# Down projection: 16 of its 22 k tiles as 7 of 8 block products, with the intermediate sums added to x1 by DMA

## The chip, the cores and the metric

One core of a Trainium2 chip runs the kernel. The metric is the device time of one execution in microseconds. Before the change it is 732.96 us, the median of 3 runs (732.8 to 734.33).

## The reference

One encoder layer over 512 positions of width 1024, all in float32. Only its last part matters here:

```python
h2 = rmsnorm(x, g_ffn)
x  = x + (silu(h2 @ w_gate) * (h2 @ w_up)) @ w_down      # w_down: 2816 x 1024
y  = rmsnorm(x, g_final)
```

Ahead of it stand an input projection, differential attention, retention in two directions, two gates and an output projection that gives the residual stream x1. The down projection is `act @ w_down`, with act of 512 x 2816: 22 k tiles of 128 along the contraction.

## The kernel before

**Split operands.** Every float32 operand of a matmul is split into a high part h (a cast to float32r, on ScalarE) and a low part l (source minus h, on VectorE). A product then takes three matmuls (h x h, h x l, l x h), all into one PSUM bank; `mm3` issues them. A weight unit is 128 x 1024: it is loaded into a buffer w_r (9 of them), cast to w_h and subtracted to w_l (4 pairs of buffers). `conv_gen` does that up to three units ahead of the matmul that uses them.

**Feed-forward groups.** `strassen` computes gate and up products of 2 x 2 blocks with seven block products in place of eight, in the order 1, 7, 6, 4, 5, 2, 3. Each product adds onto one of three pairs of banks, Y, Z and X; the intermediate values that later combinations need are copied out of PSUM by ScalarE (`snap_gen`), and the next product onto the same bank waits for that copy. The weight side of a product is a block (a, c, d) or a sum of blocks. Of the sums, t + x and s + v are formed in the buffer by an accumulating DMA issued on GpSimd's queue (POOL), t + a and t + c by a VectorE addition. Groups 0 to 4 have two units per product, group 5 is half as wide and has one. A full product is 24 matmuls of 512 columns.

**Down projection before.** For each of the 22 k tiles, one activation tile (act, 128 x 512, split into act_h and act_l by `actsplit_gen`) and one weight unit are multiplied into eight banks pd, four row tiles by two column halves: 24 matmuls per k tile. The last four k tiles run bank by bank, so that each bank ends early enough for its end work: `x2_gen` adds the bank to x1t on VectorE, then squares and gains, `final_gen` normalizes and stores.

**The order of the work** on every engine is fixed when the program is written: the class `Streams` keeps a clock for each engine with a cost for each kind of instruction, and steps the generator whose next instruction could start first; ties go to the lower rank. Each engine then runs its own queue in that order and waits on semaphores. So an instruction that is put into a queue stands in front of all that follows, whether or not it is urgent.

**Names.** fY, fZ and fX are the banks of a feed-forward group; fa4_0 to fa4_3 its four activation tiles for group 4, which `actT_gen` transposes into banks aT on the matmul engine; fg, snap_z and snap_v are values in between. S1 to S7 are the split parts that stand in for the activation side of a product. Line 90 (91 after) issues matmuls, 120 (121) casts and copies, 125 (126) VectorE additions and subtractions, 131 (132) operations with three operands, 168 (169) accumulating DMAs.

Of the kernel before, what the change touches and what calls it, by code (L numbers as in the profile page):

```python
# [36 lines left out]
class Streams:  # L37
# [184 lines left out]

@with_exitstack
def block_kernel(ctx: ExitStack, tc: tile.TileContext, xT, w_st, w_v, w_g, w_up, w_o, w_f, w_fl,
                 w_d, gc, gf, vec, cosT, sinT, posd, negd, y):

# [60 lines left out]
    for g in range(GROUPS):  # L287
        for p in PRODUCTS:
            units += [(g, p, u) for u in range(n_units(g))]
    units += [w_d[k] for k in range(FT)]  # L290
    raw, conv = {}, {}
    used = [0]
    AHEAD = 3

    def blk(g, b, u):
        return w_fl[b] if g == GROUPS - 1 else w_g[int(g[1]), b, u] if isinstance(g, str) else w_f[g, b, u]

    WARM = 9

# [552 lines left out]

    def x1t_gen():

        yield lambda: len(x1s) == KT and ("S", 0) in done
# [55 lines left out]
    def actT_gen(g, w):  # L911
        yield lambda: all((g, i) in AT for i in range(NT))
        for j in range(w // P):
            ps = yield from psum("o", f"aT{g}_{j}")
            yield from E.transposes([(ps[:, i * P:(i + 1) * P], AT[g, i][:, j * P:(j + 1) * P]) for i in range(NT)], ident)
            t = slot(f"act{g}_{j}")
            yield from E.copy(t, ps)
            E.release("o", ps)
            act32[4 * g + j] = t

    act32, usedk = {}, [0]

    def actsplit_gen():
        for k in range(FT):
            yield lambda: k in act32 and "ffn" in done and k <= usedk[0] + AHEAD
            acts[k] = yield from split(act32[k], f"act{k}")


    banks = ("w", "w", "w", "mm", "mm", "mm", "o", "o")
    gfs = []  # L930

    def gf_gen():
# [7 lines left out]
    def x2_gen(i, hf, ps, ss):  # L940

        t, u = x1t[i, hf], slot(f"u{i}{hf}")
        n = 2 if hf and i == NT - 1 else 1
        w = T // n
        for c in range(n):
            cs = slice(c * w, (c + 1) * w)
            yield from E.tt(t[:, cs], ps[:, cs], t[:, cs], ALU.add)
            if c == n - 1:
                E.release(banks[2 * i + hf], ps)
# [60 lines left out]
            for i in range(2):  # L1010
                E.spawn(v_evac_gen(pss[i], name, 2 * g + i), 15)

    def strassen(g, S, evac):

        nu = n_units(g)
        w = T * nu // 2
        per = 2 if nu == 2 else 4
        bank = {}
        for p in PRODUCTS:
            key = {"6": "n", "5": "v2", "3": "v4", "4": "z"}.get(p)  # L1020
            c = {"1": "Y", "6": "Y", "5": "Y", "3": "Y", "7": "Z", "4": "Z", "2": "X"}[p]
            first = p in "172"
            us = []
            for t in range(2):
                tag = {"Y": "mm", "Z": ("mm", "w")[t], "X": "w"}[c]
                if first:
                    bank[c, t] = (yield from psum(tag, f"f{c}{g}_{t}"))[:, :w]
                if key:
                    yield have((g, key, t))
                ps = bank[c, t]  # L1030
                for i in range(4):
                    if len(us) == i // per:
                        us.append((yield from take()))
                    uh, ul = us[i // per]
                    cs = slice((i % per) * w, (i % per + 1) * w)
                    yield lambda: (p, i) in S
                    sh, sl = S[p, i]
                    ts_ = slice(t * P, (t + 1) * P)
                    yield from E.mm3(ps, sh[:, ts_], sl[:, ts_], uh[:, cs], ul[:, cs], first and i == 0, i == 3, not first)
                    if t == 1 and i % per == per - 1:  # L1040
                        drop(us[i // per])
                if p in "1765":
                    E.spawn(snap_gen((g, {"1": "n", "7": "z", "6": "v2", "5": "v4"}[p], t), ps, w), 20)
                evac(p, t, ps, tag, w)
            if p == "7":
                done.add(("S", g))

    def main_gen():
        ps0 = []
# [101 lines left out]
        pd = {}  # L1151
        wt = {}

        def down(i, hf, k, last):
            b = 2 * i + hf
            if b not in pd:
                pd[b] = yield from psum(banks[b], f"pd{b}")
# [5 lines left out]
            yield from E.mm3(pd[b], ah[:, ts_], al[:, ts_], wt[k][0][:, cs], wt[k][1][:, cs], k == 0, last)  # L1163

        FIRST = 2
        for part in range(2):
            for k in range(FIRST):
                for i in range(2 * part, 2 * part + 2):
                    for hf in range(2):
                        yield from down(i, hf, k, False)  # L1170
                if part:
                    drop(wt.pop(k))
                    usedk[0] += 1
        for k in range(FIRST, FT - TAIL):
            for i in range(NT):
                for hf in range(2):
                    yield from down(i, hf, k, False)
            drop(wt.pop(k))
            usedk[0] += 1
        for i in range(NT):  # L1180
            ss = small([P, 3 if i == NT - 1 else 2], f"ss3_{i}")
            for hf in range(2):
                for k in range(FT - TAIL, FT):
                    yield from down(i, hf, k, k == FT - 1)
                E.spawn(x2_gen(i, hf, pd[2 * i + hf], ss), 10)
            E.spawn(final_gen(i, ss), 10)

    E.spawn(warm_gen(), 0)
# [82 lines left out]
```

## Time and profile before

| | |
|---|---|
| median of 3 runs | 732.96 us (732.8 to 734.33) |
| the profiled execution | 733.82 us, span 732.0 us |
| matmul engine (PE) | busy 715.3 us, 98% of the span, 3332 matmuls |
| VectorE (DVE) | 499.7 us, 68% |
| ScalarE (ACT) | 461.3 us, 63% |
| GpSimd (POOL) | 90.6 us, 12% |
| DMA | 98.65 MB, mean 135 GB/s |
| down projection | from 602.63 us to the last matmul, which starts at 724.26 |

A time line names engine, line, operation and tiles; a bracket at the end of a row gives how long the engine was idle before it and which engine ended that wait. The bar of a matmul is modelled and overlaps the next one, so the distance from start to start tells what it takes. On VectorE and ScalarE too, a row may begin a little before the bar of the last one ends.

### The profile page before, as it was taken

Reading aid. Unit: us, or ns where it says so; the run is one execution under the profiler, and the core shown is the slowest. Engines: PE = TensorE matmul, PEld = TensorE weight load, DVE = VectorE, ACT = ScalarE, POOL = GpSimd, SP = SyncE. Lnnn points to the kernel's source line nnn. Section 1 sums busy time; section 2 is a strip of 40 time slices with the busy share of each in tenths; the row PEclk is TensorE's granted clock in tenths of the full one; section 3 lists DMA queues with packets and bytes.
Section 4 is the critical chain, followed back from the end, with each engine's and each line's share of the span. In section 5 each row is a group of like instructions: output and inputs, shape, how many; then the busy total and the mean of one; then the engine's idle time right before and its main releaser. Section 6 shows DMA issues by size and latency. Waiting matters only on the chain.

```text
span 732.0 us, 9022 instructions
## 1 busy us (share of the span) xinstructions
PE 715.3 (98%) x3332; PEld 577.9 (79%) x3332; DVE 499.7 (68%) x704; ACT 461.3 (63%) x738; POOL 90.6 (12%) x109
## 2 busy tenths in 40 slices
PE   9989999999989999999999999999999999999995
PEld 7867677777768878887888888888888898888884
DVE  6678787779867478887577677676676864323345
ACT  7679897597696667666468866565656564223233
POOL 4261321011024002100000101000000000000000
PEclk9999999999999999999999999999999999999998
DMA  9801110311236438767604939586675563230002
GB/s 319 322 24 56 59 57 30 116 51 64 88 115 188 129 115 239 250 203 187 156 17 130 233 110 258 116 227 177 172 201 167 178 201 116 87 115 0 1 7 109
DMA packets 29052, 98.65 MB, mean 135 GB/s; under 512 B 3504, under 2 KB 3504, under 8 KB 29008
## 3 DMA queue, kind: packets, MB, share of 16 engines
q1 hardware_dynamic: 22752, 76.04, 30.3%
q0 software_dynamic: 5968, 21.50, 14.2%
q8 instruction: 26, 0.43, 0.2%
q10 hardware_dynamic: 288, 0.52, 0.2%
q14 instruction: 18, 0.15, 0.1%
HBM read 95.96 MB, written 2.10 MB: 134 GB/s over the span
## 4 chain that ended last, share of the span: by engine, by line
PE 87%; ACT 7%; DVE 4%; issue 1%; DMA 0%; SPq 0%; ACTq 0%; DVEq 0%
PE pd L90 16%; PE fY L90 15%; PE fZ L90 8%; PE wo L90 6%; PE up L90 6%; PE fYg L90 5%; PE fX L90 4%; PE pfirst L90 3%; PE rg L90 3%; PE rv L90 3%; PE fZg L90 3%; PE dv L90 2%; PE fXg L90 1%; PE s L99 1%; PE ao L90 1%; PE aT L108 1%
## 5 line engine op out<-in xcount | busy, mean ns | idle before, releaser
L125 DVE TENSOR_TENSOR w_l<-w_r,w_h 128x1024 fp32r<-128x1024 f32 (+1 forms) x66 | 76.1, 1157 | 84.3 <-ACT w_h L120 84.2
L120 ACT CAST w_h<-w_r 128x1024 fp32r<-128x1024 f32 (+1 forms) x66 | 65.6, 996 | 90.0 <-PE pd L90 61.8
L90 PE MATMUL fY<-w_h,S 128*128 128x512 f32 (+1 forms) x384 | 117.4, 376 | 0.0
L90 PEld LDWEIGHTS fY<-w_h,S 128*128 128x128 f32 x384 | 70.4, 188 | 12.1
L90 PE MATMUL fY<-w_l,S 128*128 128x512 f32 (+1 forms) x192 | 71.4, 372 | 0.0
L90 PE MATMUL pd<-w_h,act_l 128*128 128x512 f32 x176 | 68.6, 390 | 0.5 <-DVE act_l L125 0.5
L90 PE MATMUL pd<-w_l,act_h 128*128 128x512 f32 x176 | 68.6, 390 | 0.1
L90 PE MATMUL pd<-w_h,act_h 128*128 128x512 f32 x176 | 68.7, 390 | 0.0
L90 PE MATMUL fZ<-w_h,S 128*128 128x512 f32 (+1 forms) x192 | 58.9, 377 | 0.0
L90 PEld LDWEIGHTS fY<-w_l,S 128*128 128x128 f32 x192 | 36.2, 189 | 5.7
L90 PEld LDWEIGHTS fZ<-w_h,S 128*128 128x128 f32 x192 | 35.4, 188 | 6.1
L90 PEld LDWEIGHTS pd<-w_h,act_l 128*128 128x128 f32 x176 | 33.0, 188 | 7.7 <-DVE act_l L125 0.9
L90 PEld LDWEIGHTS pd<-w_l,act_h 128*128 128x128 f32 x176 | 33.0, 188 | 7.2 <-DVE w_l L125 0.6
L90 PEld LDWEIGHTS pd<-w_h,act_h 128*128 128x128 f32 x176 | 33.0, 188 | 6.8
L90 PE MATMUL fZ<-w_l,S 128*128 128x512 f32 (+1 forms) x96 | 35.6, 371 | 0.0
L90 PE MATMUL fYg<-w_h,S 128*128 128x512 f32 x96 | 31.0, 391 | 0.0
L90 PE MATMUL fX<-w_h,S 128*128 128x512 f32 (+1 forms) x96 | 28.5, 371 | 0.0
L115 ACT ACTIVATE fg<-fg,r 128x512 f32<-128x512 f32 (+1 forms) x24 | 16.2, 684 | 18.4 <-DVE fg L125 18.4
L90 PE MATMUL wo<-m_h,w_h 128*128 128x512 f32 x64 | 25.4, 397 | 0.0
L90 PE MATMUL wo<-m_l,w_h 128*128 128x512 f32 x64 | 25.1, 392 | 0.3 <-DVE m_l L125 0.2
L90 PE MATMUL wo<-m_h,w_l 128*128 128x512 f32 x64 | 24.9, 389 | 0.0
L149 DVE TENSOR_REDUCE mx<-s 128x1 f32<-128x512 f32 x32 | 21.2, 681 | 4.6 <-PE s L99 4.4
(498 smaller groups left out, 1833.5 us busy)
## 6 DMA issues: line engine op xcount, KB each, us to landing
w_r<-w_d SPq DMA_DIRECT2D x22, 512.0 KB, 3.4
w_r<-w_st SPq DMA_DIRECT2D x12, 512.0 KB, 4.5
w_r<-w_v SPq DMA_DIRECT2D x8, 512.0 KB, 5.9
w_r<-w_up SPq DMA_DIRECT2D x8, 512.0 KB, 3.3
w_r<-w_o SPq DMA_DIRECT2D x8, 512.0 KB, 4.3
x<-xT SPq DMA_DIRECT2D x8, 256.0 KB, 5.4
w(g_a)_r<-w_g SPq DMA_DIRECT2D x4, 512.0 KB, 3.7
w(g_t)_r<-w_g SPq DMA_DIRECT2D x4, 512.0 KB, 3.8
```

The source lines that it names most:

```text
L90: self.nc.tensor.matmul(out, lhsT=lhsT, rhs=rhs, start=start, stop=stop, skip_group_check=more)
L99: self.nc.tensor.matmul(outs[i % 2], lhsT=lhsT, rhs=rhs, start=i < 2, stop=i >= len(ops) - 2)
L108: self.nc.tensor.transpose(out=out, in_=in_, identity=identity)
L115: self.nc.scalar.activation(out, in_, func, **kw)
L120: self.nc.scalar.copy(out=out, in_=in_)
L125: (self.nc.vector if eng == "dve" else self.nc.gpsimd).tensor_tensor(out=out, in0=a, in1=b, op=op)
L149: self.nc.vector.tensor_reduce(out=out, in_=a, axis=AX.X, op=op, **kw)
```

## The change

The first 16 k tiles become two groups, d0 and d1, of eight k tiles each. Each is a 2 x 2 block product done with `strassen`: the four row tiles and the eight k tiles are halved, and the weight blocks lie in a new array w_db, prepared ahead of the launch. `dblocks_gen` makes the seven activation-side parts from eight act tiles (28 splits of 128 x 256 and 16 additions or subtractions of 128 x 256 per group): those of d0 during group 5, those of d1 during d0. `down_evac_gen` copies an intermediate bank out of PSUM into a tile cd, with its sign, and adds that tile to x1t by an accumulating DMA on POOL's queue: 12 such copies and adds in d0, 8 in d1. Bank pair X stays and takes d1's product 2 on top of d0's; d1 puts Y into the two banks of tag o. The last six k tiles (REST) run as all 22 did before, onto six banks that d1 leaves and two new ones. Since rows of the lower half are formed with their sign turned, the act tiles from 16 on have their second half negated, and `x2_gen` subtracts for row tiles 2 and 3.

```diff
+REST = 6
...
-    units += [w_d[k] for k in range(FT)]
+    units += [(g, p, u) for g in ("d0", "d1") for p in PRODUCTS for u in range(2)]
+    units += [w_d[k] for k in range(REST)]
...
-    def dma_add(self, out, in_):
-        yield "pool", [out]
+    def dma_add(self, out, in_, sbuf_in=False):
+        yield "pool", [out, in_] if sbuf_in else [out]
         self.nc.gpsimd.dma_start(out=out, in_=in_, accum_op=ALU.add)
...
+    def dblocks_gen(g):
+        k0 = 8 * int(g[1])
+        prev = "d0" if g == "d1" else GROUPS - 1
+        store = Sd[g]
+        yield lambda: all(k0 + n in act32 for n in range(8))
+        a = [act32.pop(k0 + n) for n in range(8)]
+        w, w2 = {}, {}
+        yield have(("P", prev - 1, "2") if g == "d0" else ("P", prev, "1"))
+        for i in range(4):
+            yield from part(store, "1", i, a[i][:, A])
+        for i in range(4):
+            w[i] = slot(f"dsum{g}{i}")
+            yield from E.tt(w[i][:, A], a[i][:, A], a[i][:, B], ALU.add)
+            yield from part(store, "7", i, w[i][:, A])
...
+    def down_evac_gen(g, p, t, ps, tag):
+        key, i, hf, op = {"1": ("n", t, 0, ALU.subtract), "7": ("z", 2 + t, 1, ALU.add), "6": ("v2", 2 + t, 0, ALU.add),
+                          "4": (None, 2 + t, 0, ALU.subtract), "5": ("v4", 2 + t, 1, ALU.subtract),
+                          "3": (None, t, 1, ALU.add), "2": (None, 0, 0, None)}[p]
+        if key or op and g == "d0":
+            c = slot(f"c{g}{p}{t}")
+            if op == ALU.add:
+                yield from E.copy(c, ps)
+            else:
+                yield from E.act(c, ps, AF.Copy, scale=-1.0)
+            if key:
+                done.add((g, key, t))
+            else:
+                E.release(tag, ps)
+            yield from E.dma_add(x1t[i, hf], c, sbuf_in=True)
...
+        bank = {}
+        for g in ("d0", "d1"):
+            def evac(p, t, ps, tag, w):
+                E.spawn(down_evac_gen(g, p, t, ps, tag), 9)
+            if g == "d1":
+                for c in "YZ":
+                    for t in range(2):
+                        bank.pop((c, t))
+            yield from strassen(g, Sd[g], evac, TAGS if g == "d0" else {**TAGS, "Y": ("o", "o")}, bank)
+        pd = {(t, 0): bank["X", t] for t in range(2)}
+        pd.update({(t, 1): bank["Y", t] for t in range(2)})
+        pd.update({(2 + t, 0): bank["Z", t] for t in range(2)})
+        wt, onto = {}, set(pd)
...
-        for k in range(FIRST, FT - TAIL):
+        for k in range(FT - REST, FT - TAIL):
```

In the program's order the matmul engine's queue goes from 3317 rows to 3269, VectorE's from 704 to 796. Up to the end of group 4 the queues are the same.

VectorE's queue at the end of group 4, where group 5's first units are split and combined (w139, w140, w(5_0_t)) and the last two activation tiles of group 4 are made (fa4_0, fa4_1), before:

```order
L125 TENSOR_TENSOR w139_l_5311<-w(5_0_t)_r_5139,w139_h_5310 128x1024
L125 TENSOR_TENSOR w(5_0_t)_r_5139<-w(5_0_t)_r_5139,w(5_0_a)_r_5093 128x1024
L131 SCALAR_TENSOR_TENSOR fa4_0_5321<-fY4_0_5017,r2_95,fg4_0_5278 128x512
L125 TENSOR_TENSOR w140_l_5332<-w(5_0_t)_r_5139,w140_h_5331 128x1024
L125 TENSOR_TENSOR w(5_0_t)_r_5139<-w(5_0_t)_r_5139,w(5_0_c)_r_5179 128x1024
L131 SCALAR_TENSOR_TENSOR fa4_1_5341<-fY4_1_5038,r2_95,fg4_1_5301 128x512
```

and now:

```order
L126 TENSOR_TENSOR w139_l_5314<-w(5_0_t)_r_5139,w139_h_5313 128x1024
L126 TENSOR_TENSOR w(5_0_t)_r_5139<-w(5_0_t)_r_5139,w(5_0_a)_r_5093 128x1024
L126 TENSOR_TENSOR S1_0_5299<-act0_0_4071,S1_0_5299 128x256
L126 TENSOR_TENSOR S1_1_5341<-act0_1_4085,S1_1_5341 128x256
L126 TENSOR_TENSOR S1_2_5344<-act0_2_4097,S1_2_5344 128x256
L132 SCALAR_TENSOR_TENSOR fa4_0_5325<-fY4_0_5017,r2_95,fg4_0_5277 128x512
L126 TENSOR_TENSOR w140_l_5336<-w(5_0_t)_r_5139,w140_h_5335 128x1024
L126 TENSOR_TENSOR w(5_0_t)_r_5139<-w(5_0_t)_r_5139,w(5_0_c)_r_5179 128x1024
L126 TENSOR_TENSOR S1_3_5348<-act0_3_4114,S1_3_5348 128x256
L126 TENSOR_TENSOR dsumd00_5385<-act0_0_4071 128x256
L132 SCALAR_TENSOR_TENSOR fa4_1_5352<-fY4_1_5038,r2_95,fg4_1_5300 128x512
```

Five rows of d0's parts now stand ahead of fa4_1.

VectorE's queue where the weights for product 4 of d0 are made (units w151 and w152; S2, S1 and dsum are parts of d0 and d1), after the change:

```order
L132 SCALAR_TENSOR_TENSOR w151_l_5816<-w(d0_0_t)_r_5261,w151_h_5815 128x1024
L126 TENSOR_TENSOR w(d0_1_t)_r_5302<-w(d0_1_t)_r_5302,w(d0_1_c)_r_5399 128x1024
L126 TENSOR_TENSOR S2_1_5836<-act1_1_4409,S2_1_5836 128x256
L126 TENSOR_TENSOR S2_2_5867<-act1_2_4421,S2_2_5867 128x256
L126 TENSOR_TENSOR S2_3_5870<-act1_3_4438,S2_3_5870 128x256
L126 TENSOR_TENSOR dsum2d00_5694<-act1_0_4395,dsumd00_5385 128x256
L126 TENSOR_TENSOR S1_3_5838<-act2_3_4762,S1_3_5838 128x256
L126 TENSOR_TENSOR dsumd10_5881<-act2_0_4719 128x256
L132 SCALAR_TENSOR_TENSOR w152_l_5857<-w(d0_1_t)_r_5302,w152_h_5856 128x1024
```

Between the addition into w(d0_1_t) and w152_l stand six rows of parts. VectorE's queue around the units of the same numbers before the change:

```order
L125 TENSOR_TENSOR w151_l_5769<-w151_r_5408,w151_h_5768 128x1024
L125 TENSOR_TENSOR act7_l_5805<-act1_3_4438,act7_h_5804 128x512
L125 TENSOR_TENSOR w152_l_5803<-w152_r_5465,w152_h_5802 128x1024
L125 TENSOR_TENSOR act8_l_5839<-act2_0_4719,act8_h_5838 128x512
L125 TENSOR_TENSOR w153_l_5837<-w153_r_5499,w153_h_5836 128x1024
```

There, splits of weights (w_l) and of activation tiles (act_l) alternate, without an addition.

POOL's queue in d0, after the change (cd06 and cd04 are the copies of products 6 and 4, the last digit the half; before, the queue ends with the two loads of gf):

```order
L169 DMA x1t20_3851<-cd060_5842 128x512
L169 DMA x1t30_3903<-cd061_5865 128x512
L169 DMA x1t20_3851<-cd040_5907 128x512
L169 DMA w(d1_0_t)_r_5889<-w_db 128x1024
L169 DMA w(d1_1_t)_r_5936<-w_db 128x1024
L169 DMA x1t30_3903<-cd041_5934 128x512
```

The accumulating loads of d1's weights stand behind adds into x1t; the second add into x1t20 may be issued only when the first has landed.

## Rows read from the trace of the kernel before

**Rows 1.** The page, busy us of each engine with its share of the span
```profile
PE 715.3 (98%) x3332; PEld 577.9 (79%) x3332; DVE 499.7 (68%) x704; ACT 461.3 (63%) x738; POOL 90.6 (12%) x109
```

**Rows 2.** Stretches of 40 us: a feed-forward group, the down projection; columns in its head
```profile
core 0: us, PE busy (x) PEld busy (x) DVE busy (x) ACT busy (x) POOL busy (x), PEclk, DMA share, GB/s
468.00:508.00 40.00, 40.00 (x186) 33.14 (x186) 27.87 (x30) 23.59 (x32) 3.49 (x4) 1.00 0.68 185
604.00:644.00 40.00, 40.00 (x181) 33.07 (x181) 15.06 (x19) 14.39 (x21) 0.00 (x0) 1.00 0.32 106
```

**Rows 3.** The chain of waits: start us, us, what
```profile
558.70 5.44 PE fZ L90 x24
...
585.30 0.44 PE aT L108 x4
...
588.39 2.88 PE fY L90 x24
...
605.81 96.62 PE pd L90 x426
```

**Rows 4.** Time line of PE: start us, us, what, idle before it and releaser
```profile
583.68 0.55 PE L108 MATMUL aT<-ident,fa 128*128 128x128 f32 x3 [0.24 <-DVE fa L131]
...
602.63 0.40 PE L90 MATMUL pd<-w_h,act_h 128*128 128x512 f32 x1
602.86 0.40 PE L90 MATMUL pd<-w_l,act_h 128*128 128x512 f32 x1
603.73 0.50 PE L90 MATMUL pd<-w_h,act_l 128*128 128x512 f32 x1 [0.47 <-DVE act_l L125]
```

**Rows 5.** Time line of DVE at the end of group 4
```profile
575.05 0.69 DVE L125 TENSOR_TENSOR fg<-fX,snap_n 128x512 f32<-128x512 f32 x1 [1.22 <-PE fX L90]
575.66 1.22 DVE L125 TENSOR_TENSOR w_l<-w(5_0_a)_r,w_h 128x1024 fp32r<-128x1024 f32 x1
576.79 1.22 DVE L125 TENSOR_TENSOR w_l<-w(5_0_t)_r,w_h 128x1024 fp32r<-128x1024 f32 x1
578.05 1.23 DVE L125 TENSOR_TENSOR w(5_0_t)_r<-w(5_0_t)_r,w(5_0_a)_r 128x1024 f32<-128x1024 f32 x1
579.19 0.74 DVE L131 SCALAR_TENSOR_TENSOR fa<-fY,r,fg 128x512 f32<-128x512 f32 x1
580.47 1.23 DVE L125 TENSOR_TENSOR w_l<-w(5_0_t)_r,w_h 128x1024 fp32r<-128x1024 f32 x1 [0.54 <-ACT w_h L120]
...
582.88 0.74 DVE L131 SCALAR_TENSOR_TENSOR fa<-fY,r,fg 128x512 f32<-128x512 f32 x1
```

**Rows 6.** Time line of DVE ahead of group 0, rows that follow without a wait
```profile
380.90 1.22 DVE L125 TENSOR_TENSOR w(0_0_t)_r<-w(0_0_t)_r,w(0_0_a)_r 128x1024 f32<-128x1024 f32 x1
382.04 0.42 DVE L125 TENSOR_TENSOR S<-sum,S 128x256 fp32r<-128x256 f32 x1
382.37 0.42 DVE L125 TENSOR_TENSOR sum<-sum,hs 128x256 f32<-128x256 f32 x1
```

**Rows 7.** ACT by line and shape: count, busy us, mean ns of one, idle before
```profile
L120 ACT CAST w_h<-w_r 128x1024 fp32r<-128x1024 f32 x22 | 23.1, 1052 | 69.1 <-PE pd L90 61.8 <-issue 6.3 <-ACT snap_v L120 1.0
L120 ACT COPY snap_v<-fY 128x512 f32<-128x512 f32 x16 | 9.4, 585 | 12.0 <-PE fY L90 12.0
L120 ACT CAST S<-hs 128x256 fp32r<-128x256 f32 x4 | 1.6, 404 | 0.0
```

**Rows 8.** The page, DMA queues: packets, MB, share of 16 engines over the span
```profile
q1 hardware_dynamic: 22752, 76.04, 30.3%
q0 software_dynamic: 5968, 21.50, 14.2%
```

**Rows 9.** Line 168's accumulating loads of 512 KB: issue on POOL, time to landing
```profile
L168 POOL DMA_DIRECT2D w(4_0_t)_r<-w_f x1: 872/872/872, 522.7 to 522.7; - x1
...
DMA to landing us min/median/max: 5.3/7.4/14.4
```

**Rows 10.** Tile xr, plain loads of 256 KB by POOL's queue: time to landing
```profile
DMA to landing us min/median/max: 6.4/7.7/8.7
```

More of the change, by code (lines that the diff above doesn't have):

```diff
@@ L224, in block_kernel @@
 def block_kernel(ctx: ExitStack, tc: tile.TileContext, xT, w_st, w_v, w_g, w_up, w_o, w_f, w_fl,
-                 w_d, gc, gf, vec, cosT, sinT, posd, negd, y):
+                 w_db, w_d, gc, gf, vec, cosT, sinT, posd, negd, y):
     nc = tc.nc
@@ L295, in blk @@
     def blk(g, b, u):
-        return w_fl[b] if g == GROUPS - 1 else w_g[int(g[1]), b, u] if isinstance(g, str) else w_f[g, b, u]
+        if isinstance(g, str):
+            return (w_g if g[0] == "g" else w_db)[int(g[1]), b, u]
+        return w_fl[b] if g == GROUPS - 1 else w_f[g, b, u]
     WARM = 9
@@ L853, in x1t_gen @@
     def x1t_gen():
-        yield lambda: len(x1s) == KT and ("S", 0) in done
+        yield lambda: len(x1s) == KT and ("P", 0, "7") in done
         for i in range(NT):
@@ L916, in actT_gen @@
             t = slot(f"act{g}_{j}")
-            yield from E.copy(t, ps)
+            if 4 * g + j < FT - REST:
+                yield from E.copy(t, ps)
+            else:
+                yield from E.copy(t[:, A], ps[:, A])
+                yield from E.act(t[:, B], ps[:, B], AF.Copy, scale=-1.0)
             E.release("o", ps)
@@ L923, in actsplit_gen @@
     def actsplit_gen():
[L924 to L929, printed above, removed]
+        for k in range(FT - REST, FT):
+            yield lambda: k in act32 and ("P", "d1", "1") in done and k <= FT - REST + usedk[0] + AHEAD
+            acts[k] = yield from split(act32.pop(k), f"act{k}")
+    Sd = {"d0": {}, "d1": {}}
+    def dblocks_gen(g):
[12 more added lines that the diff above has]
+            yield from part(store, "7", i, w[i][:, A])
+        yield have(("P", prev, "1"))
+        for i in range(4):
+            yield from E.tt(w[i][:, A], w[i][:, A], a[4 + i][:, B], ALU.subtract)
+            yield from part(store, "6", i, w[i][:, A])
+        yield have(("P", prev, "7"))
+        for i in range(4):
+            yield from part(store, "4", i, a[4 + i][:, B])
+        yield have(("P", prev, "6"))
+        for i in range(4):
+            w2[i] = slot(f"dsum2{g}{i}")
+            yield from E.tt(w2[i][:, A], a[4 + i][:, B], a[i][:, B], ALU.subtract)
+            yield from part(store, "5", i, w2[i][:, A])
+        yield have(("P", prev, "4"))
+        for i in range(4):
+            yield from part(store, "2", i, a[4 + i][:, A])
+        yield have(("P", prev, "5"))
+        for i in range(4):
+            yield from E.tt(w2[i][:, B], a[4 + i][:, A], w[i][:, A], ALU.subtract)
+            yield from part(store, "3", i, w2[i][:, B])
@@ new lines, in down_evac_gen @@
+    def down_evac_gen(g, p, t, ps, tag):
[10 more added lines that the diff above has]
+                done.add((g, key, t))
+            else:
+                E.release(tag, ps)
+            yield from E.dma_add(x1t[i, hf], c, sbuf_in=True)
@@ L946, in x2_gen @@
             cs = slice(c * w, (c + 1) * w)
-            yield from E.tt(t[:, cs], ps[:, cs], t[:, cs], ALU.add)
-            if c == n - 1:
-                E.release(banks[2 * i + hf], ps)
+            yield from E.tt(t[:, cs], t[:, cs], ps[:, cs], ALU.add if i < 2 else ALU.subtract)
             sq = slot(f"sq3_{i}{hf}{c}")[:, :w]
@@ L1011, in proj_v, with strassen @@
                 E.spawn(v_evac_gen(pss[i], name, 2 * g + i), 15)
-    def strassen(g, S, evac):
+    TAGS = {"Y": ("mm", "mm"), "Z": ("mm", "w"), "X": ("w", "w")}
+    def strassen(g, S, evac, tags=TAGS, bank=None):
         nu = n_units(g)
@@ L1017, in strassen @@
         per = 2 if nu == 2 else 4
-        bank = {}
+        bank = {} if bank is None else bank
         for p in PRODUCTS:
@@ L1021, in strassen @@
             c = {"1": "Y", "6": "Y", "5": "Y", "3": "Y", "7": "Z", "4": "Z", "2": "X"}[p]
-            first = p in "172"
             us = []
             for t in range(2):
-                tag = {"Y": "mm", "Z": ("mm", "w")[t], "X": "w"}[c]
+                first = (c, t) not in bank
                 if first:
-                    bank[c, t] = (yield from psum(tag, f"f{c}{g}_{t}"))[:, :w]
+                    bank[c, t] = (yield from psum(tags[c][t], f"f{c}{g}_{t}"))[:, :w]
                 if key:
@@ L1041, in strassen, with snaps_of @@
                         drop(us[i // per])
[L1042 to L1046, printed above, removed]
+                evac(p, t, ps, tags[c][t], w)
+            done.add(("P", g, p))
+    def snaps_of(g, p, t, ps, w):
+        if p in "1765":
+            E.spawn(snap_gen((g, {"1": "n", "7": "z", "6": "v2", "5": "v4"}[p], t), ps, w), 20)
     def main_gen():
@@ L1109, in evac @@
             def evac(p, t, ps, tag, w):
+                snaps_of(g, p, t, ps, w)
                 if p == "4":
@@ L1138, in evac @@
             def evac(p, t, ps, tag, w):
+                snaps_of(g, p, t, ps, w)
                 if p == "4":
@@ L1149, in main_gen @@
         done.add("ffn")
-        pd = {}
-        wt = {}
+        bank = {}
[11 more added lines that the diff above has]
+        wt, onto = {}, set(pd)
         def down(i, hf, k, last):
-            b = 2 * i + hf
-            if b not in pd:
-                pd[b] = yield from psum(banks[b], f"pd{b}")
+            first = (i, hf) not in pd
+            if first:
+                pd[i, hf] = yield from psum("mm", f"pd{i}{hf}")
             if k not in wt:
@@ L1162, in down @@
             ts_, cs = slice(i * P, (i + 1) * P), slice(hf * T, (hf + 1) * T)
[L1163 to L1173, printed above, removed]
-        for k in range(FIRST, FT - TAIL):
+            yield from E.mm3(pd[i, hf], ah[:, ts_], al[:, ts_], wt[k][0][:, cs], wt[k][1][:, cs], first, last, (i, hf) in onto)
+        for k in range(FT - REST, FT - TAIL):
             for i in range(NT):
@@ L1184, in main_gen @@
                     yield from down(i, hf, k, k == FT - 1)
-                E.spawn(x2_gen(i, hf, pd[2 * i + hf], ss), 10)
+                E.spawn(x2_gen(i, hf, pd[i, hf], ss), 10)
             E.spawn(final_gen(i, ss), 10)
@@ L1198, in block_kernel @@
     E.spawn(actsplit_gen(), 3)
+    for g in ("d0", "d1"):
+        E.spawn(dblocks_gen(g), 8)
     E.spawn(gf_gen(), 50)
@@ L1217 @@
     inp = {n: np.asarray(a) for n, a in inputs.items()}
-    w_in = inp["w_in"][0]
+    w_in, wd = inp["w_in"][0], inp["w_ffn_down"][0]
     def stationary(w):
@@ L1250 @@
         "w_fl": quarters(slice(5 * T, 5 * T + T // 2), T // 2)[:, :, 0].transpose(0, 2, 1, 3).reshape(4, P, 2 * T),
-        "w_d": inp["w_ffn_down"][0].reshape(FT, P, D),
+        "w_db": np.stack([quarters(slice(0, T), T, (wd[c * D:(c + 1) * D, :T], wd[c * D:(c + 1) * D, T:]))
+                          .reshape(4, 2, 2, P, T).transpose(0, 1, 3, 2, 4).reshape(4, 2, P, 2 * T) for c in range(2)]),
+        "w_d": wd[2 * D:].reshape(REST, P, D),
         "gc": np.concatenate([cols(inp["g_mix"][0]), cols(inp["g_ffn"][0]), cols(inp["g_final"]),
```

## The prediction

> **What bounds the kernel now.** I read the page's busy times first: TensorE (PE) is busy for 98% of the span [rows 1]. An average over stages could hide a gap, so the table of stretches came next: in a full feed-forward group and in the down projection PE is busy 40.00 us of 40.00, while VectorE (DVE) falls from 27.87 to 15.06 and ScalarE (ACT) from 23.59 to 14.39 [rows 2]. The reader is to see that there is no time but matmul time, and that the stage which changes is the one with the most idle DVE. Third, the chain of waits: 24 matmuls of 512 columns take 5.44 us, and 426 of the down projection 96.62, both 0.2267 us each; in the half-wide group 5 a product takes 2.88, and four transposes 0.44 [rows 3]. Last, PE's own waits at the two seams of group 5, in the time line: a transpose that waits for a DVE row at 583.68, and the down projection's third matmul, which begins 0.87 after the second instead of 0.23 [rows 4].
>
> **The change part by part.** *Matmuls.* Before: 22 k tiles x 8 banks x 3 = 528. After: two groups of 7 x 2 x 4 x 3 = 168, and six k tiles of 24, 480 in all. 48 x 0.2267 = 10.88 us less, all on the path. The transposes stay. The late third matmul waited for the split of an activation; d0's first product takes parts that were split during group 5, so 0.64 goes as well.
>
> *What the 10.88 is paid with.* For d0: 14 weight splits (22 served the whole down projection before), four weight additions, 28 splits of 256 columns, 16 additions of 256 columns and 12 copies out of PSUM. DVE rows that follow each other without a wait start 1.14 apart (1024 columns) and 0.335 apart (256) [rows 6]. That is 18 x 1.14 + 44 x 0.335 = 35.3 us of DVE for 38.1 us of PE, where a feed-forward group had 27.87 in 40. ACT: 14 x 1.05 + 12 x 0.59 + 28 x 0.40 = 33 us at most [rows 7]. Both fit, DVE barely, and its queue is in order. So I walked DVE's order through the three places where PE waits for it.
>
> *First place, the end of group 4.* Before, fa4_0 starts at 579.19 and fa4_1 at 582.88 [rows 5]. Now three 256-wide rows stand ahead of fa4_0: 579.19 + 1.0 = 580.2. It takes 0.65 (its 0.74 less the overlap of 0.085), so the next split starts at 580.85 instead of 580.47 (0.54 of idle time swallows most of the push). The addition behind it starts 1.26 later, as from 576.79 to 578.05, since it overwrites what the split reads: 582.11, then 583.25; two more 256-wide rows: fa4_1 at 583.92, 1.04 late. PE's transpose waits for it, so everything on PE is 1.04 late: d0 begins at 602.63 + 1.05 = 603.7.
>
> *Second place, aT5 in d0's first product.* The transposes stand nine matmuls into d0, at 605.7. DVE's walk on (fa4_1 584.6, group 5's splits as PE frees their buffers, the last at about 602.7, five rows to fa5_1) ends at 605.8. No slack: every further lateness of DVE shows. I allow 0.6.
>
> *Third place, product 4 of d0 and of d1.* With 8 transposes (0.88) the products of d0 end at 610.0, 615.4 and 620.9. In product 4 the second unit's weights are t + c: addition on DVE, cast on ACT, residual on DVE. ACT comes to w151_h after the copy that waits for product 7's end at 615.4, two casts and its own 1.05: 617.7. DVE: w151_l from 617.7 (1.2: a 1024-wide row 1.14, and a three-operand row of 512 takes 0.74 against 0.69 [rows 5]), the addition from 619.0, six 256-wide rows from 620.1 to 622.1, and only then w152_l, done at 623.4. PE wants it six matmuls into product 4, at 620.9 + 1.36 + 0.23 = 622.5: 0.9 late. In d1 two 256-wide rows stand there instead of six, but four splits of 512 columns earlier in the chain; the same walk gives 0.5. Elsewhere the weights are ready 2 to 5 us ahead. Where the walk is wrong both ways: PE had no wait in a feed-forward group [rows 2], so 0 from below; from above the rival on DVE's bars.
>
> *Copies and DMA adds.* A copy has from one product's end to the one after the next, 8 us for a row of 0.59; only ACT's order could hold it. The 20 adds into x1t are read by the end stage alone, and the last two are issued some 35 us before they are read (product 5 of d1 ends near 671, the bank that needs them near 710). Nearest rows: 256 KB by POOL's queue landed in 6.4 to 8.7 us [rows 10], accumulating loads of 512 KB in 5.3 to 14.4, POOL's part 0.87 [rows 9]. I take 8, and 0 us on the path.
>
> *The end stage.* The last six k tiles, the last four weights' buffers and the tail after the last matmul keep their order: 0.
>
> Sum: -10.88 - 0.64 + 1.04 + 0.6 + 0.9 + 0.5 = -8.5 us. The profiled execution took 733.82 (span 732.0), so 725.3; the median of the runs, 732.96, lies 0.86 below it: **724.5**.
>
> **The rivals.** *DVE keeps up.* If none of the last three waits appears and fa4_1's does not either, -10.88 - 0.64 = -11.5: 721.4. For it: rows 2. Against: 35.3 us instead of 27.87, and the five rows ahead of fa4_1 stand in the order.
>
> *DVE is as slow as its bars.* If every DVE row takes its whole bar (1.22 and 0.42) and not the distance of starts, each costs 0.085 more. 48 rows lie between 575.66 and fa5_1, which has no slack: 4.1 us instead of the 0.6 I allow, and some ten rows in each product 4 add 0.9 twice. 3.5 + 1.8 = 5.3: 729.8. The load of d0 would be 18 x 1.22 + 44 x 0.42 = 40.4 us, over PE's 38.1. Rows 6 speak against it (0.335 between starts of 0.42 bars); rows that wait for a cast or for the row before (578.05) speak for a part. The Trainium skill (VectorE: DVE Perf Modes, The DRAIN you can't avoid) says that the next VectorE operation starts only when the pipe is empty, with an exception for one that is not held; this trace shows mostly the exception.
>
> *The weight add behind the x1t adds, slower than before.* On POOL the add into w(d1_0_t) now stands behind x1t20<-cd040, which waits until x1t20<-cd060 has landed. cd060's add is issued at about 619.7 (product 6, first half, ends at 618.2; copy 0.6; POOL 0.87). With a landing time L the weight is complete at 619.7 + 2L + 1.74; ACT's cast of it is wanted at 646.5 (product 7 of d1 at 648.9 less cast and residual 2.4), and everything behind that cast on ACT waits too. It bites from L = 12.5, costs 3.7 us at 14.4, and eats the whole gain, 8.5, at L = 16.8; beyond that, at 18 say, 735. For it: the DMA engines. A MB costs 0.303 x 732 / 76.04 = 2.92 us on the loads' queue and 0.142 x 732 / 21.50 = 4.83 on POOL's [rows 8]; d0's ten loads, four weight adds and twelve x1t adds are 5.24 x 2.92 + 5.24 x 4.83 = 40.6 us of a 38.1 us stage, so landings will stretch. Against: much of it may spill into the six plain k tiles, whose loads are half as dense, and about 8 is the usual landing. The Trainium skill (DMA: Bandwidth & Descriptors, Anatomy of one DMA) fits 2.0 us + bytes/436e3 for a DMA issued from GpSimd, an estimate of 2.6 us for 256 KB. By it this rival would have no chance at all; no row here is that short, and rows 9 and 10 decide.
>
> **How the numbers follow.** Forecast 68% (its own range 721.8 to 726.5), DVE keeps up 8%, DVE as slow as its bars 16% (727 to 731), the late weight add 8%, half of it beyond the old time. The range 721.6 to 729.0 leaves out some of the first rival's half, most of the bars' upper half and the late add. A difference of 0.2%, 1.5 us, is about what a measurement of this kernel can tell from no change. All cases but the late add lie more than that below 732.96: faster 0.94, same 0.02, slower 0.04.
>
> **What the profile of the changed kernel would show.** Right: 48 matmuls fewer at the same 0.2267; a PE wait of about 1.3 before aT4's second transpose, released by fa4_1; none on PE at the start of d0 but perhaps aT5's; a wait on w152_l, and a smaller one on w166_l; x1t adds landing in 6 to 10 us with nobody waiting. Wrong: PE waits on a DMA or on ACT's copies, weight adds landing beyond 12 us, DVE starts 0.42 apart in d0, or a sum of PE waits between 575 and the last matmul over 7 us.

## The result, and the profile after

The changed kernel takes **725.97 us**, the median of 4 runs (725.54 to 726.41), against 732.88 of the kernel before in the same comparison: ratio 0.9901 (worked out from all runs, not from the two medians), 95% interval 0.9884 to 0.9918. The forecast was 724.5 with a range of 721.6 to 729.0. The profiled executions are 8.1 us apart (733.82 and 725.72) and their spans 8.5 us (732.0 and 723.5), the size that the sum gave; the medians are 6.9 apart. On a second chip they were 8.6 apart (below).

The page after, busy times and DMA queues, against [rows 1, 8]:

```profile
PE 705.2 (97%) x3284; PEld 568.7 (79%) x3284; DVE 542.3 (75%) x796; ACT 493.3 (68%) x816; POOL 114.5 (16%) x137
...
q1 hardware_dynamic: 23328, 78.14, 30.7%
q0 software_dynamic: 10000, 30.94, 21.5%
```

The stretches of 40 us, columns as in [rows 2]:

```profile
468.00:508.00 40.00, 40.00 (x188) 33.19 (x186) 27.87 (x29) 23.59 (x31) 3.45 (x4) 1.00 0.66 185
604.00:644.00 40.00, 39.23 (x178) 32.01 (x177) 35.33 (x61) 29.18 (x53) 11.32 (x14) 1.00 0.83 212
```

PE fell by 10.1 us busy, a little less than 10.88: some 0.3 of the difference lies ahead of the change (X of group 4 starts 0.32 later, below), and around a wait the bars count more than the distance of starts (0.50 at 623.87 for 0.2267). In the first stretch nothing changed. In the second, DVE went from 15.06 to 35.33, and PE has idle time there for the first time.

The time line of PE at the four places where it waits or was expected to, against [rows 4]:

```profile
583.48 0.27 PE L109 MATMUL aT<-ident,fa 128*128 128x128 f32 x1
585.04 0.55 PE L109 MATMUL aT<-ident,fa 128*128 128x128 f32 x3 [1.28 <-DVE fa L132]
...
603.99 0.40 PE L91 MATMUL fYd<-w_h,S 128*128 128x512 f32 x1
604.22 0.40 PE L91 MATMUL fYd<-w_l,S 128*128 128x512 f32 x1
604.46 0.62 PE L91 MATMUL fYd<-w_h,S 128*128 128x512 f32 x2
...
606.06 0.67 PE L109 MATMUL aT<-ident,fa 128*128 128x128 f32 x4
606.49 0.48 PE L91 MATMUL fYd<-w_h,S 128*128 128x512 f32 x1
...
622.71 0.39 PE L91 MATMUL fZd<-w_h,S 128*128 128x512 f32 x1
623.87 0.50 PE L91 MATMUL fZd<-w_l,S 128*128 128x512 f32 x1 [0.77 <-DVE w_l L132]
...
662.75 0.50 PE L91 MATMUL fZd<-w_l,S 128*128 128x512 f32 x1 [0.46 <-DVE w_l L132]
```

At the second of these places the four transposes into aT take 0.43 to the next matmul (606.06 to 606.49). Before, the same four took 0.36:

```profile
604.07 0.60 PE L108 MATMUL aT<-ident,fa 128*128 128x128 f32 x4
604.43 0.48 PE L90 MATMUL pd<-w_h,act_h 128*128 128x512 f32 x1
```

What a wait costs is read from the starts: 623.87 - 622.71 is 1.16 where 0.2267 would do, so 0.93 is lost, though the bracket says 0.77. In d1 the same working from the start at 662.75 gives 0.63, for a bracket of 0.46. The last matmul starts at 715.94 instead of 724.26, 8.32 earlier. X of group 4, ahead of anything that the change does, starts 0.32 later than before in this execution (569.73 for 569.41).

DVE at the end of group 4, against [rows 5]:

```profile
578.37 1.23 DVE L126 TENSOR_TENSOR w(5_0_t)_r<-w(5_0_t)_r,w(5_0_a)_r 128x1024 f32<-128x1024 f32 x1
579.51 1.09 DVE L126 TENSOR_TENSOR S<-act,S 128x256 fp32r<-128x256 f32 x3
580.51 0.75 DVE L132 SCALAR_TENSOR_TENSOR fa<-fY,r,fg 128x512 f32<-128x512 f32 x1
581.18 1.22 DVE L126 TENSOR_TENSOR w_l<-w(5_0_t)_r,w_h 128x1024 fp32r<-128x1024 f32 x1
582.43 1.22 DVE L126 TENSOR_TENSOR w(5_0_t)_r<-w(5_0_t)_r,w(5_0_c)_r 128x1024 f32<-128x1024 f32 x1
583.57 0.42 DVE L126 TENSOR_TENSOR S<-act,S 128x256 fp32r<-128x256 f32 x1
583.90 0.42 DVE L126 TENSOR_TENSOR dsumd<-act 128x256 f32<-128x256 f32 x1
584.24 0.75 DVE L132 SCALAR_TENSOR_TENSOR fa<-fY,r,fg 128x512 f32<-128x512 f32 x1
```

The two rows at 583.57 and 583.90 are d0's parts that stand ahead of fa4_1. The walk had fa4_1 at 583.92; with the 0.32 of this execution that is the 584.24 of the last row.

DVE ahead of product 4 of d0:

```profile
619.45 1.22 DVE L126 TENSOR_TENSOR w(d_t)_r<-w(d_t)_r,w(d_c)_r 128x1024 f32<-128x1024 f32 x1
620.58 1.09 DVE L126 TENSOR_TENSOR S<-act,S 128x256 fp32r<-128x256 f32 x3
621.59 0.42 DVE L126 TENSOR_TENSOR dsum2d<-act,dsumd 128x256 f32<-128x256 f32 x1
621.92 0.42 DVE L126 TENSOR_TENSOR S<-act,S 128x256 fp32r<-128x256 f32 x1
622.26 0.42 DVE L126 TENSOR_TENSOR dsumd<-act 128x256 f32<-128x256 f32 x1
622.60 1.22 DVE L132 SCALAR_TENSOR_TENSOR w_l<-w(d_t)_r,w_h 128x1024 fp32r<-128x1024 f32 x1
```

and ACT's cast that w152_l needs:

```profile
620.76 1.06 ACT L116 ACTIVATE w_h<-w(d_t)_r 128x1024 fp32r<-128x1024 f32 x1 [0.73 <-DVE w(d_t)_r L126]
```

The cast is done at 621.8, and w152_l starts at 622.60: the last 0.8 is due to the six rows of parts, not to the cast. From group 4 on, none of PE, VectorE and ScalarE waits for a DMA in this trace; only POOL does, ahead of accumulating weight loads. The x1t adds land in 3.3 / 7.0 / 14.2 us (least, median, most), where the forecast had 6 to 10.

### The profile page after: what moved, and what is told of

Its sections match the earlier page's. It is cut to its first block, busy times and chain, and to the rows that moved or that the text cites. A ratio compares the mean times of both kernels' runs of the same rounds, so it can differ in the third digit from the quotient of the medians.

```text
span 723.5 us, 9200 instructions
## 1 busy us (share of the span) xinstructions
PE 705.2 (97%) x3284; PEld 568.7 (79%) x3284; DVE 542.3 (75%) x796; ACT 493.3 (68%) x816; POOL 114.5 (16%) x137
## 4 chain that ended last, share of the span: by engine, by line
PE 84%; ACT 7%; DVE 6%; issue 1%; DMA 0%; SPq 0%; ACTq 0%; DVEq 0%
PE fY L91 16%; PE fZ L91 8%; PE wo L91 6%; PE up L91 6%; PE fYd L91 5%; PE fYg L91 5%; PE fX L91 4%; PE pfirst L91 3%; PE rg L91 3%; PE rv L91 3%; PE fZd L91 3%; PE fZg L91 3%; PE fXd L91 2%; PE dv L91 2%; PE fXg L91 2%; PE s L100 1%
## 5 line engine op out<-in xcount | busy, mean ns | idle before, releaser
L126 DVE TENSOR_TENSOR w_l<-w_r,w_h 128x1024 fp32r<-128x1024 f32 (+1 forms) x50 | 56.6, 1136 | 30.7 <-ACT w_h L121 30.2
L121 ACT CAST w_h<-w_r 128x1024 fp32r<-128x1024 f32 (+1 forms) x50 | 48.8, 980 | 34.6 <-issue 8.1
L91 PE MATMUL fYd<-w_h,S 128*128 128x512 f32 x128 | 41.1, 391 | 0.0
L91 PEld LDWEIGHTS fYd<-w_h,S 128*128 128x128 f32 x128 | 24.0, 188 | 4.9
L91 PE MATMUL fYd<-w_l,S 128*128 128x512 f32 x64 | 24.9, 389 | 0.0
L169 POOL DMA_DIRECT2D x1t<-cd x20 | 18.0, 932 | 43.8 <-ACT cd L116 21.5
L116 ACT ACTIVATE e<-s,mx 128x512 f32<-128x512 f32 x32 | 21.9, 687 | 2.1 <-DVE mx L150 1.7
L121 ACT COPY snap_v<-fY 128x512 f32<-128x512 f32 (+1 forms) x24 | 13.2, 550 | 12.0 <-PE fY L91 12.0
```

Source lines behind the costliest of these rows:

```text
L91: self.nc.tensor.matmul(out, lhsT=lhsT, rhs=rhs, start=start, stop=stop, skip_group_check=more)
L116: self.nc.scalar.activation(out, in_, func, **kw)
L121: self.nc.scalar.copy(out=out, in_=in_)
L126: (self.nc.vector if eng == "dve" else self.nc.gpsimd).tensor_tensor(out=out, in0=a, in1=b, op=op)
```

## The experiments

Except where it is said, an experiment is compared with the kernel before on its own chip. The median of the kernel before is 733.91 to 734.31 on the three chips of the experiments and 732.88 in the comparison above, so ratios are given. A time inside the trace is counted from the start of X of group 4 to the start of the last matmul: 154.85 us before, 146.20 in the changed kernel's repeat, 8.65 less.

**The changed kernel again**, on a second chip, beside the runs without the DMA adds, with d0's parts later and with every add doubled; the others ran on two more chips.

> The changed kernel again, beside the others on one chip. Theory A (48 matmuls less, minus three waits of the matmul engine for VectorE's queue): 0.990 of the time before, 7 to 8.5 us less. The profile again shows waits of about 1.3 us at the first transposes of group 4, 0.8 us at product 4 of d0 and 0.5 us at product 4 of d1. Theory B (the DMA adds into x1t cost time, by POOL's queue or by DMA bandwidth): the same time, so this run alone tells nothing apart; it is the base for the others.

725.69 us (725.36 to 726.5), ratio 0.9881 (0.9861 to 0.99). The waits are the same three, 1.28, 0.77 and 0.46.

**Without the DMA adds.** The 20 adds into x1t are left out, so x1 lacks those sums.

```diff
-            yield from E.dma_add(x1t[i, hf], c, sbuf_in=True)
```

> The 20 DMA adds of intermediate sums into x1t are left out (the sums are still copied out of PSUM), so the result lacks them. The queues of the matmul engine, VectorE and ScalarE keep their order. Theory A: within 0.3 us of the changed kernel, and the same three waits. Theory B: faster than the changed kernel by 1 us or more, with weight loads that land earlier and shorter waits.

726.02 us, ratio 0.9885 (0.9865 to 0.9904); 146.27 in the trace. Its row of 604 to 642, columns as in the stretches above:

```profile
604.00:642.00 38.00, 37.18 (x168) 30.36 (x167) 34.34 (x59) 27.58 (x52) 1.85 (x3) 1.00 0.55 163
```

The same row with the adds:

```profile
604.00:642.00 38.00, 37.23 (x172) 30.58 (x171) 34.59 (x58) 28.22 (x51) 11.29 (x13) 1.00 0.82 205
```

POOL falls from 11.29 to 1.85 and the DMA share from 0.82 to 0.55, and PE stays where it was. The adds cost nothing that these runs can tell.

**Without DVE's 16 additions per group.**

```diff
-            w[i] = slot(f"dsum{g}{i}")
-            yield from E.tt(w[i][:, A], a[i][:, A], a[i][:, B], ALU.add)
-            yield from part(store, "7", i, w[i][:, A])
+            yield from part(store, "7", i, a[i][:, B])
... (so too for products 6, 5 and 3)
```

> Leaves out the 16 additions of 128 x 256 per group (the split parts of products 7, 6, 5 and 3 are taken from single tiles, so sums are missing in the output); all matmuls, splits, copies and DMA adds stay. In VectorE's order one row fewer stands ahead of fa4_1 (four instead of five) and three instead of six rows between the second weight addition and w152_l of d0; in d1 none instead of two. Theory A (what the change pays is VectorE's queue, rows of parts standing ahead of urgent ones): the wait before aT4's second transpose falls by one row, from 1.28 to about 0.95, the wait on w152_l in d0 from 0.77 to 0 to 0.2, the one on w166_l in d1 from 0.46 to 0, together 1.3 to 1.6 us below the changed kernel. Theory B (the residual of product 4 is late because ScalarE casts late, and VectorE only waits with it): both waits stay, and the time is within 0.4 us of the changed kernel.

723.93 us, ratio 0.9861 (0.9848 to 0.9873); 144.30, that is 1.90 less than the changed kernel. PE's only wait from 568 to the end:

```profile
585.74 0.55 PE L109 MATMUL aT<-ident,fa 128*128 128x128 f32 x3 [0.95 <-DVE fa L132]
```

One row of 0.335 fewer ahead of fa4_1 took 0.33 off its wait, and both waits of product 4 are gone. 0.33 + 0.93 + 0.63 is 1.89. Theory A, with a size that was too small because I had added the brackets and not the starts. This run takes rows off VectorE and so lightens its load too; the next one changes the order alone.

**d0's parts only after group 4's transposes.** Nothing is left out; one wait in the planner's order.

```diff
-        yield have(("P", prev - 1, "2") if g == "d0" else ("P", prev, "1"))
+        yield (lambda: all((prev - 1, i) in AT for i in range(NT))) if g == "d0" else have(("P", prev, "1"))
```

> The first parts of d0 are made only after the four activation tiles of group 4, so none of them stands ahead of fa4_1 in VectorE's queue. Theory A: the wait at group 4's transposes falls from 1.3 us to the 0.2 of before; 1.0 us of that may come back where VectorE has no slack (fa5_1 before aT5, product 4 of d0), so 0.3 to 1.5 us faster than the changed kernel. Theory C (the wait is only moved: VectorE's work between 575 and 623 us is the limit): within 0.2 us of the changed kernel, with waits at aT5 or at w152 longer by as much as the first is shorter.

723.87 us (722.36 to 724.18), ratio 0.9851 (0.983 to 0.9871), the lowest ratio of all, though the version without additions lies inside its interval; 144.40, 1.80 less, more than the 1.5 that was expected at most. PE's waits:

```profile
582.87 0.55 PE L109 MATMUL aT<-ident,fa 128*128 128x128 f32 x3 [0.23 <-DVE fa L132]
638.53 0.73 PE L91 MATMUL fYd<-w_h,S 128*128 128x512 f32 x2 [0.47 <-DVE S L126]
```

The late fa4_1 is gone, as was expected. Both waits of product 4 went as well: with another start of the parts the planner put three rows in place of six ahead of w152_l, and w151_l came 1.55 earlier (47.01 after the start of X of group 4, for 48.56). In their place a part of product 3 in d0 is late by 0.47 (a later expectation calls it product 2).

**One group only.** REST is 14: d0 is a block product, 14 k tiles run as before.

> Only d0 is a block product; the other 14 k tiles run as all 22 did before: 504 matmuls in the down projection instead of 528 before and 480 after. Theory A (each saved matmul is worth its 0.2267 us, the late fa4_1 is paid once, at the end of group 4, and product 4's wait is paid by each group as VectorE's order has it): -24 x 0.2267 - 0.64 + 1.04 = -5.0 us, and with three instead of six rows ahead of w152_l a wait there of 0 to 0.2: 4.8 to 5.0 us below the kernel before, that is 3.5 us above the changed kernel. Theory B (the two groups share the costs evenly, as they would if crowding of VectorE or of the DMA engines cost in proportion to the work): half of the changed kernel's gain, about 4.1 us below before and 4.1 above the changed one. Theory C (d0 and d1 crowd each other, so that one group alone costs nothing): -5.44 - 0.64 = 6.1 us below before.

729.45 us, ratio 0.994 (0.9928 to 0.9952); 150.20, 4.65 below before. PE's waits:

```profile
586.31 0.55 PE L109 MATMUL aT<-ident,fa 128*128 128x128 f32 x3 [1.28 <-DVE fa L132]
624.53 0.50 PE L91 MATMUL fZd<-w_l,S 128*128 128x512 f32 x1 [0.17 <-DVE w_l L132]
```

Theory A by its places: the late fa4_1 in full, and a wait on w152_l that costs 0.33 by the starts, with the 0.07 of aT5: -5.44 - 0.64 + 1.04 + 0.07 + 0.33 = -4.64. The time by itself could not tell: A gave 4.8 to 5.0, half of 8.65 would be 4.33, and the measured 4.65 lies between them.

**Every add doubled.** A second add of 256 KB from the same copy behind each of the 20, into four extra tiles in turn.

```diff
+            junk.append(junk.pop(0))
+            yield from E.dma_add(junk[-1], c, sbuf_in=True)
```

> Each of the 20 adds is followed by a second one of the same tile into one of four scratch tiles, which four plain loads of 256 KB set up; the result is unchanged. VectorE's order is unchanged. Theory A: the adds are read late and the weight add behind them had about 4 us to spare, so 0 to 2 us slower than the changed kernel; if slower, the place is product 7 of d1, waiting through ScalarE's cast of w161 for the weight add. Theory B: at least 3 us slower, spread over both groups.

732.01 us (730.79 to 734.8), ratio 0.9967 (0.9953 to 0.9981): 6.3 us above the changed kernel. Theory A, that the adds have ample room, is wrong at twice their number; the place that it named, ScalarE's casts for product 7 of d1, comes back below. The next four ask why.

**The four extra tiles alone**: loaded, without the second adds.

> Control for the doubled adds: the four extra tiles are taken and loaded, but no second add is issued. The order on every engine is as in the changed kernel but for the four loads. Theory A (the second adds themselves cost): within 0.5 us of the changed kernel. Theory B (four tiles fewer, or their loads, cost): 3 us or more above it.

726.18 us, ratio 0.9885 (0.9872 to 0.9899). Tiles and loads cost nothing.

**Second adds from a constant tile**, so that no copy is held for them. The constant tile is a fifth extra one.

```diff
-            yield from E.dma_add(junk[-1], c, sbuf_in=True)
+            yield from E.dma_add(junk[3], junk[4], sbuf_in=True)
```

> As the doubled adds (a second accumulating DMA of 256 KB behind each of the 20), but the second add reads one constant tile and not the copy cd, so that no copy's buffer is held until a second add lands. Theory A (in the doubled version the extra 6.3 us came from ScalarE, whose copies and casts waited for buffers that the second adds still held): at most 1.5 us above the changed kernel. Theory B (they came from the adds' traffic and from the accumulating weight loads of d1, which stand behind them in GpSimd's queue and land late): 4 to 7 us above the changed kernel, with PE waiting for w_l and w_h of d1's products 7, 6 and 4 from about 650 us on, and landings of some 13 us as in the doubled version.

732.43 us, ratio 0.9979 (0.9962 to 0.9996). Held copies are not the reason: theory B.

**The second adds in d0 only, and in d1 only.**

```diff
+            if g == "d0":    # or "d1"
                 yield from E.dma_add(junk[3], junk[4], sbuf_in=True)
```

> The second add from a constant tile only behind the 12 adds of d0. Theory A (the late piece is d1's weight sum t + x of product 7, whose accumulating loads stand in GpSimd's queue behind d0's adds and land later, so that ScalarE's casts of w(d1_0_t) and w(d1_1_t) come late): nearly all of the 6.3 us that doubling all 20 cost, 5 to 6.5 us above the changed kernel, with both casts waiting for their loads. Theory B (transfers crowd the DMA engines wherever they lie, and the cost goes with their number): 12 of 20, 3 to 4.5 us. Theory C (it is the adds in d1, beside d1's own weights, that cost): at most 1.5 us.

> The second add only behind the 8 adds of d1, all of them issued behind the two loads of product 7's weight sum. Theory A: within 0.8 us of the changed kernel, no wait on the casts of w(d1_0_t) and w(d1_1_t); the sums s + v of product 5 stand behind the new adds, but have some 10 us more. Theory B: 8 of 20, 2 to 3 us above. Theory C: 5 us or more above.

In d0: 730.17 us, ratio 0.9949 (0.9936 to 0.9961), 150.48 in the trace, 4.28 above the changed kernel. In d1: 725.09 us, ratio 0.9881 (0.9869 to 0.9894), 146.41. So eight more transfers in d1 are free and twelve in d0 cost 4 to 5 us. ACT's casts of w(d1_0_t) and w(d1_1_t) with the second adds in d0:

```profile
645.58 1.05 ACT L121 CAST w_h<-w(d_t)_r 128x1024 fp32r<-128x1024 f32 x1 [2.79 <-DMA w(d_t)_r<-w_db]
649.29 1.05 ACT L121 CAST w_h<-w(d_t)_r 128x1024 fp32r<-128x1024 f32 x1 [2.35 <-DMA w(d_t)_r<-w_db]
```

In d1:

```profile
643.57 1.05 ACT L121 CAST w_h<-w(d_t)_r 128x1024 fp32r<-128x1024 f32 x1 [0.51 <-ACT S L121]
644.92 1.06 ACT L121 CAST w_h<-w(d_t)_r 128x1024 fp32r<-128x1024 f32 x1
```

The time of d0 by itself could not tell: theory A gave 5 to 6.5 above, theory B 3 to 4.5. That d1 costs nothing, and the two casts, speak for A's place.

This is the place of the third rival: the accumulating load of d1's first sum comes late. But it is not late by its place in POOL's queue. The issues of these loads, with the second adds in d0:

```profile
633.76 0.87 POOL L169 DMA_DIRECT2D w(d_t)_r<-w_db  x1 [2.06 <-DVE S L126]
636.41 0.86 POOL L169 DMA_DIRECT2D w(d_t)_r<-w_db  x1 [1.78 <-DMA w(d_t)_r<-w_db]
```

The second of them with the second adds in d1:

```profile
631.67 0.87 POOL L169 DMA_DIRECT2D w(d_t)_r<-w_db  x1 [0.48 <-DVE w_l L126]
```

With the second adds in d0 POOL stands idle ahead of both loads, and what ends its wait at 636.41 is the plain load of t into the same buffer, which comes by SyncE's queue. That load, issued at 625.6 and 625.8 in the two runs, lands after 10.3 us with the second adds in d0 and after 5.3 with them in d1; the accumulating load is issued 0.5 to 0.6 us behind that landing in both, and then takes 12.8 us against 11.4. So loads on both queues land later while the second adds of d0 move, and most of the extra delay is on the queue that holds no add. In d1 the first second add is issued at 649.03, six us after these loads have landed.

Not all of the 4.28 is waiting. PE in product 6 of d1, with the second adds in d0:

```profile
657.48 0.50 PE L91 MATMUL fYd<-w_h,S 128*128 128x512 f32 x1 [0.32 <-ACT w_h L121]
659.35 0.69 PE L91 MATMUL fYd<-w_l,S 128*128 128x512 f32 x1 [1.37 <-DVE w_l L126]
659.84 1.05 PE L91 MATMUL fYd<-w_h,S 128*128 128x512 f32 x2
660.70 0.63 PE L91 MATMUL fYd<-w_l,S 128*128 128x512 f32 x1
```

By the starts the two waits lose 2.1; the nine matmuls from 659.35 to 663.10 lose 1.7 more, since most start 0.43 apart (granted clock 0.88 from 650 to 664, 1.00 in the changed kernel's repeat).

Doubling in both groups costs some 2 us more than in d0 alone, though d1 alone costs nothing; how the two add up stays open.

**A version meant to beat both**: the third edit of this list, and every step of the parts taken by the planner as 0.6 us later than it could start.

```diff
-                t = self.start(*s[3])
+                t = self.start(*s[3]) + (self.HOLD if s[0] == 8 else 0.0)
```

> A version that may beat both: d0's parts start only when group 4's four activation tiles are transposed (as in the third experiment), and the planner takes every step of the parts as 0.6 us later than it could start, so that weights go ahead of parts where both are ready. In VectorE's order three rows stand between the second weight addition and w152_l in d0, and the one or two that stood before w166_l in d1 stay. Theory A (every wait that is left is a row of parts ahead of an urgent row): the wait of 0.47 on a part of product 2 in d0 is what is left to win or lose; 0 to 0.6 us below the third experiment, 1.8 to 2.4 below the changed kernel. Theory B (parts that are put off come late themselves, since VectorE has little room in d0): PE waits on parts S by 1 us or more, and the time is between the changed kernel and 2 us above it.

740.98 us (740.22 to 745.36), ratio 1.0094 (1.008 to 1.0109), slower than before. Neither theory's number: it is theory B's mechanism, far larger. The trace is of the slowest of its five runs, 4.4 us above the median. PE in product 6 of d0:

```profile
618.51 0.50 PE L92 MATMUL fYd<-w_h,S 128*128 128x512 f32 x1 [1.11 <-ACT S L122]
...
620.46 0.49 PE L92 MATMUL fYd<-w_h,S 128*128 128x512 f32 x1 [1.22 <-DVE S L127]
621.57 0.50 PE L92 MATMUL fYd<-w_h,S 128*128 128x512 f32 x1 [0.62 <-ACT S L122]
...
622.87 1.57 PE L92 MATMUL fYd<-w_h,S 128*128 128x512 f32 x2 [0.57 <-DVE S L127]
624.24 0.63 PE L92 MATMUL fYd<-w_l,S 128*128 128x512 f32 x1
624.67 1.05 PE L92 MATMUL fYd<-w_h,S 128*128 128x512 f32 x2
625.52 0.63 PE L92 MATMUL fYd<-w_l,S 128*128 128x512 f32 x1
```

and its stretches:

```profile
604.00:642.00 38.00, 32.74 (x120) 23.20 (x119) 31.03 (x59) 24.66 (x49) 8.67 (x10) 0.88 0.71 160
642.00:681.00 39.00, 35.51 (x137) 27.23 (x136) 28.30 (x48) 23.76 (x43) 9.59 (x11) 0.90 0.84 184
```

PE now waits for the parts themselves, ten times: seven waits, 6.1 us by the brackets, end with a cast of a part on ScalarE, and three, 2.4 us, with its residual on VectorE. Both engines are less busy from 604 to 642 (DVE 31.03, ACT 24.66) than in the version without the 0.6 (35.02 and 29.50), and still late. That speaks for the order that holds PE up and not the load, on ScalarE more than on VectorE. That the weights had fewer rows ahead of them in the order said nothing of when the parts would be due.

## Why the prediction was right

- **Matmuls, -10.88.** 48 fewer at 0.2267, in blocks of 24 that still take 5.44 us. Right.
- **The third matmul of the down projection, -0.64.** In d0 it starts 0.24 after the second. Right.
- **First place, 1.04.** 585.04 - 583.68 - 0.32 = 1.04. The run without additions took one row away and got its 0.335 back, the run with later parts got the whole back. Right.
- **Second place, 0.6 allowed.** Measured 0.07, 0.43 for 0.36 (above). The walk's end was right (605.8 + 0.32, and DVE's last fa ends at about 606.1), and that was just in time; the allowance for further lateness was not needed.
- **Third place, 0.9 and 0.5.** Measured 0.93 and 0.63. In d0 the six rows are the main cause. In d1 DVE itself waits 0.52 for ACT's cast ahead of the late residual, so there the two rows are not what ends last. That the lateness comes down the chain from the splits of 512 columns, as the walk had it, is argued; no run takes these splits away.
- **Copies and adds, 0.** Right, as the run without the adds shows, but with less room than I gave it. I had asked only when the first of d1's two sums is wanted. The second is tighter: in the repeat its load was issued at 633.77, landed 10.9 later at 644.67, and its cast began at 645.29. That leaves 0.6 us; in the first trace 2.7 (631.17 + 10.6, cast at 644.46).

The waits sum to 2.67 for the forecast 3.04; -10.88 - 0.64 + 2.67 + 0.32 = -8.53, where the last matmul moved by -8.32; 0.2 I can't place. The profiled execution was forecast at 725.3 and took 725.72. That the median is 1.5 above 724.5 comes mostly from the last step: the profiled execution before lay 0.86 above the median of its runs, and I took that off; the one after lies 0.25 below its own. In the later runs the profiled execution lies on either side as well, 0.5 above its median in the repeat and 1.5 below in the version with later parts. That step took scatter for an offset. The interval of the ratio leaves room for a gain of 6.0 to 8.5 us, so the medians neither confirm nor refute the last 1.5 of the sum; the traces and the second chip do the confirming.

**The rivals.** DVE keeps up (721.4): the three waits are there, so no; the later parts show that 1.8 us of the difference can be had by order alone. DVE as slow as its bars (729.8): parts start 0.33 to 0.34 apart in the changed kernel too, with bars of 0.42 (583.57, 583.90, 584.24 above). The Trainium skill (VectorE: DVE Perf Modes, The DRAIN you can't avoid) would have each start when the one before has drained; the trace again shows the exception that it allows. The late weight add: it did not happen, though in the repeat only 0.6 us of slack was left. The rival had half of it: its ground, that landings stretch when the DMA engines are full, is what the second adds in d0 showed; its chain, an add that waits for the one before it in POOL's queue, is not what made the load late. Where d0's adds were doubled, x1t's landed in 13.6 to 14.8 us by the median, and it cost 4 to 7 us of the 8.6; the rival gave 3.7 for 14.4. That the sizes agree is luck, since the chain was another and part of the cost was PE's clock. The Trainium skill (DMA: Bandwidth & Descriptors, Anatomy of one DMA) gives for 256 KB an estimate of 2.6 us; the traces here have a least of 3.3 and a median of 7.0, and by that fit neither rival nor experiment would have lost anything.

## What to carry to other kernels

Walk the order of the engine that fills up, row by row, to the few places where the bound engine waits for it: loads that "fit" still put rows ahead of urgent ones, and each row that counted cost its distance of starts. For a transfer that costs nothing, find the tightest load that moves beside it, on any queue, and state the slack in us; a free step with 0.6 us of slack is not a safe one. And when an order is changed to spare one deadline, list the other deadlines that it moves.

## What the runs showed of the hardware

Waiting cost twice. In the version with the 0.6 the granted clock, 1.00 over the same stretches in the changed kernel and in the version without the 0.6, was 0.88 and 0.90, and after four waits between 617 and 623 us matmuls start 0.43 apart (624.24 to 624.67, and two from there to 625.52) instead of 0.2267, which is the lower of the two levels, 1.2 for 2.4 GHz (granted clock 0.50 from 624 to 629). From X of group 4 to the last matmul this version took 164.16 us in that execution, 19.8 more than the version without the 0.6, while PE's idle time in the two stretches grew by 8.2 only (5.26 + 3.49, for 0.47 + 0.12). The version with the second adds in d0 shows the same on a smaller scale, after two waits within 2 us. In the changed kernel, whose waits are single and at most 1.28 us, the granted clock stayed at 1.00 in these stretches.
